# A two-layer model's second modulation: products on GpSimd, or multiply-adds on VectorE

## The chip, the cores and the metric

The kernel runs on one core of one Trainium2 chip. The metric is the device time of one execution in microseconds (us). The kernel before was timed three times: 3883.1, 3865.46 and 3878.24 us, median 3878.24 us. One more execution, of 3871.71 us, was recorded with the hardware profiler; its span is 3870.0 us and all rows below come from it.

The engines are named as the profile names them: PE is TensorE (matmuls and transposes), PEld its weight loads, DVE is VectorE, ACT is ScalarE, POOL is GpSimd, SP is SyncE, which here issues most DMA transfers. Each engine takes its instructions in one fixed order. L821 is line 821 of the kernel.

## The reference, cut to what matters

512 tokens of width 1024 go through two layers. Both end in a mixture of experts with 16,384 experts. The second layer is modulated by a vector `c`, and its attention is partly a differential one:

```python
mod = jax.nn.silu(c) @ w_ada + b_ada              # c: 1024, w_ada: 1024 x 6144
sh1, sc1, g1, sh2, sc2, g2 = split(mod, 6)        # six rows of 1024
h = rms_norm(x, norm1_g) * (1 + sc1) + sh1
proj = h @ w_in                                   # attention inputs and gate logits gl
...
a = softmax(q1 k1^T / 8) - lam * softmax(q2 k2^T / 8)     # 8 heads, 512 x 512 each
ob = rms_norm(a @ v, subln_g) * (1 - lam_init)
gates = sigmoid(gl + b_gate)
x = x + g1 * (mixed @ w_out)
h2 = rms_norm(x, norm2_g) * (1 + sc2) + sh2
x = x + g2 * experts(h2)
```

Only the making of `mod` is touched. Its rows sh1, sc1 and g1 (0 to 2) are made early, beside the first layer's mixture of experts; rows sh2, sc2 and g2 (3 to 5) beside the differential attention. They are first read after that attention has ended.

## The kernel before, in words

**A modulation row** is a product of a vector with a 1024 x 1024 block of `w_ada`. `modulation` (L788) does it without PE for the most part. It loads the block in eight pieces of 128 x 1024 (tile `war`, 512 KB each, two buffers in turn), multiplies each piece with one column of silu(c) (tile `cc`, one value a partition) and adds it into the tile `am`. Then `finish` (L797) sums `am` over the partitions by eight small matmuls against a column of ones (`pmod`, L800), adds the bias (`bada`, L803), turns the result by one transpose (`ptmod`, L806) and stores it to DRAM (`modd`, L809). There is one buffer of `am` and one of `bada`, so a row's first piece can't be written before the matmuls of the row before it have read `am`.

The function has two ways to form `am`. With `on_pool` false a piece takes one DVE instruction, a tensor-scalar product for the first piece (L823) and a fused multiply-add for the other seven (L825), and SP issues the loads. With `on_pool` true POOL issues the loads (L816), and a piece takes a product (L819) and, from the second piece on, a sum (L821), both on POOL. The first call (rows 0 to 2, L1423) is of the first kind, the second call (rows 3 to 5, L1655) of the second.

**The differential attention** (L1608) runs eight times, over four blocks of 128 tokens and two halves of four heads. A pass splits its queries in a high and a low part (`qbhi`, `qblo`), and for each head and each of the two softmaxes makes scores by three matmuls of 512 columns (`bps`, L118 to L120), a row maximum on DVE (`nm`, L746) and an exponential on ACT (`pe`, L748). DVE scales and subtracts the two (L1627, L1630), PE transposes the difference (`bpt`, L1633), ACT copies it, and PE multiplies it with the values (`bpo`, L1637). A normalization follows, whose last step is the only other POOL instruction of the stage (L1646).

Each pass is followed in the program by `projT` (L1590), which makes 256 columns of the gate logits: eight weight pieces of 128 x 256 (`wr`, three buffers) are loaded by SP, split by ACT and DVE in two parts (`wh`, `wl`, L76 and L77), and used by 48 matmuls of 512 columns (`mt`, L1601 to L1603). After each pass the loop asks the modulation for four steps (L1660).

**The order of the work.** The program is written in this order, but a scheduler lays each engine's instructions out anew, by its own estimate of when their inputs will be there. So the gate matmuls stand between the attention's, on PE, and the splits between the softmax steps, on DVE. The order is fixed when the kernel is built. What runs after the stage (sigmoids of the gates, the projections, the second mixture of experts) reads the results of all of it.

Of the kernel before, what the change touches and what calls it, by code (L numbers as in the profile page):

```python
# [23 lines left out]
def build(tc, I, out, dbg=None, stop=None):  # L24
# [763 lines left out]
    def modulation(rows, pool, psum, tags, ptag, on_pool):  # L788

        cc = pool.tile([128, 8], F32, name="cc", bufs=1)  # L790
        S.dma_start(out=cc, in_=I["c_2"])
        A.activation(out=cc, in_=cc, func=AF.Silu)
        ones = pool.tile([128, 1], F32, name="ones", bufs=1)
        G.memset(ones, 1.0)
        mv = modd.rearrange("(i d) -> i d", d=128)

        def finish(i, am):  # L797
            pm = psum.tile([128, 8], F32, name="pmod", tag=ptag)
            for j in range(8):
                T.matmul(pm[:, j:j + 1], am[:, j * 128:(j + 1) * 128], ones, start=True, stop=True)  # L800
            b8 = pool.tile([128, 8], F32, name="bada", tag="bada", bufs=1)
            S.dma_start(out=b8, in_=I["k_bada"][:, i * 8:i * 8 + 8])
            V.tensor_tensor(out=b8, in0=pm, in1=b8, op=OP.add)  # L803
            yield
            pt = psum.tile([128, 128], F32, name="ptmod", tag=ptag)
            T.transpose(pt[0:8, :], b8, ident)  # L806
            mrow = pool.tile([8, 128], F32, name="mrow", tag="mrow", bufs=1)
            A.copy(out=mrow, in_=pt[0:8, :])
            S.dma_start(out=mv[i * 8:i * 8 + 8], in_=mrow)  # L809
            yield  # L810

        for i in rows:
            am = pool.tile([128, 1024], F32, name="am", tag=tags[0])
            for k in range(8):
                raw = pool.tile([128, 1024], F32, name="war", tag=tags[1], bufs=None if tags[1] == "row" else 2)
                (G if on_pool else S).dma_start(out=raw, in_=I["w_ada_2"][k * 128:(k + 1) * 128, i * 1024:(i + 1) * 1024])  # L816
                ck = cc[:, k:k + 1]
                if on_pool:
                    G.tensor_tensor(out=raw if k else am, in0=raw, in1=ck.broadcast_to([128, 1024]), op=OP.mult)  # L819
                    if k:  # L820
                        G.tensor_tensor(out=am, in0=am, in1=raw, op=OP.add)  # L821
                elif k == 0:
                    V.tensor_scalar(out=am, in0=raw, scalar1=ck, scalar2=None, op0=OP.mult)  # L823
                else:
                    V.scalar_tensor_tensor(out=am, in0=raw, scalar=ck, in1=am, op0=OP.mult, op1=OP.add)  # L825
                yield
            for _ in range(ML):
                yield
            yield from finish(i, am)
# [12 lines left out]
    MR = (0, 1, 2)  # L842
# [809 lines left out]
        return f  # L1652

    modp = dp.enter_context(tc.tile_pool(name="modp", bufs=1))
    mods = modulation(tuple(range(len(MR), 6)), modp, pst, ("am", "war"), "tr", True)  # L1655
    for t in range(NT):
        for h4 in range(2):
            differential(t, h4)
# [220 lines left out]
```

## Time and profile before

| | |
|---|---|
| median of three runs | 3878.24 us (3865.46 to 3883.1) |
| the profiled execution | 3871.71 us |
| its span | 3870.0 us |
| the stage of the change, from PE's first `bps` to the last row's `ptmod` | 2183.8 to 2430.8 us, 247.0 us |
| PE busy in the span | 3667.4 us (95%) |
| DVE, POOL busy in the span | 3028.6 us (78%), 1915.2 us (49%) |

The profile is one execution, cut in several ways: busy time by engine, groups of instructions by line with their mean duration, what each engine waited for, and the instructions in order of time. PE's matmuls overlap, and their ends are modelled, so a PE that counts as busy may still run below its peak; for its progress the count of its instructions in a stretch is the better measure. The granted clock (PEclk) is the share of full speed that PE was given in a stretch.

### The profile page before, as it was taken

The numbers are of one execution on the slowest core, as the hardware profiler recorded it, in microseconds if no ns is written. First come the engines' busy times: TensorE is split into PE (matmuls) and PEld (weight loads), VectorE is DVE, ScalarE is ACT, GpSimd is POOL, SyncE is SP. The second block draws the span as 40 slices with busy tenths as digits, with TensorE's granted clock in tenths as the row PEclk, the third lists the DMA queues.
The fourth block names the chain that finished last, engine by engine and source line by source line (L and its number), as shares of the span: only waits on it lengthen the run. The fifth ranks groups of instructions, "written<-read, shape, count | busy, mean of one in ns | idle before, by whom it ended". The sixth has DMA issues, their size and how long they took to land. (4 is left out here: it accounts for less than half of the span.)

```text
span 3870.0 us, 53220 instructions
## 1 busy us (share of the span) xinstructions
PE 3667.4 (95%) x19062; PEld 3166.8 (82%) x19062; DVE 3028.6 (78%) x5530; ACT 1654.5 (43%) x2567; POOL 1915.2 (49%) x1261
## 2 busy tenths in 40 slices
PE   6999999899999999999899988999899999999999
PEld 4777788788899999987777666788788899999987
DVE  8557479996898888877756566589996898888775
ACT  3455433475333333333444566433474333333333
POOL 3000047514778887740524443147524778877740
PEclk8999999999999999999999989999999999999999
DMA  3423132257999899987222322432257999999884
GB/s 110 108 91 120 55 120 88 95 217 266 324 335 327 318 321 322 325 300 249 81 80 65 93 75 71 134 112 88 93 219 271 325 337 327 321 317 323 306 280 147
DMA packets 333513, 789.03 MB, mean 204 GB/s; under 512 B 32432, under 2 KB 152320, under 8 KB 329856
## 3 DMA queue, kind: packets, MB, share of 16 engines
q1 hardware_dynamic: 256064, 504.58, 39.6%
q0 software_dynamic: 77184, 281.05, 20.3%
q8 instruction: 150, 2.46, 0.3%
q14 instruction: 115, 0.94, 0.1%
HBM read 725.34 MB, written 59.01 MB: 203 GB/s over the span
## 5 line engine op out<-in xcount | busy, mean ns | idle before, releaser
L1104 POOL TENSOR_TENSOR ul<-ur,uh 128x1024 fp32r<-128x1024 f32 x256 | 696.3, 2720 | 436.6 <-PE pa L1114 251.5
L1111 PE MATMUL pa<-phi,uh 128*128 128x384 f32 x2048 | 698.1, 341 | 1.5 <-ACT ga L1116 1.5
L1112 PE MATMUL pa<-plo,uh 128*128 128x384 f32 x2048 | 695.7, 340 | 0.0
L1305 PE MATMUL y<-vh,wh 128*128 128x512 f32 x1536 | 596.7, 393 | 15.6 <-ACT wh L1274 13.8
L1306 PE MATMUL y<-vl,wh 128*128 128x512 f32 x1536 | 600.3, 392 | 5.6 <-DVE vl L1276 5.6
L1307 PE MATMUL y<-vh,wl 128*128 128x512 f32 x1536 | 602.4, 394 | 0.0
L1276 DVE TENSOR_TENSOR vl<-vr,vh 128x1024 fp32r<-128x1024 f32 x256 | 359.5, 1404 | 210.6 <-ACT vh L1275 182.6
L1274 ACT CAST wh<-w 128x384 fp32r<-128x384 f32 x256 | 131.4, 513 | 764.1 <-PE y L1306 523.9
L1251 DVE SCALAR_TENSOR_TENSOR acc<-vrow,act,acc 128x1024 f32<-128x1024 f32 x256 | 408.4, 1595 | 56.5 <-DMA vrow<-in_peer_v_dram,ei 28.4
L1240 DVE SCALAR_TENSOR_TENSOR urow<-urow,hgat 128x1024 f32<-128x1024 f32 x256 | 407.6, 1599 | 29.2 <-DMA urow<-in_peer_u_dram,ei 17.2
L1114 PE MATMUL pa<-phi,ul 128*128 128x384 f32 x2048 | 402.8, 339 | 16.5 <-POOL ul L1104 16.4
L1098 ACT CAST uh<-ur 128x1024 fp32r<-128x1024 f32 x256 | 269.6, 1053 | 317.6 <-issue 211.1
L1111 PEld LDWEIGHTS pa<-phi,uh 128*128 128x128 f32 x2048 | 389.3, 190 | 10.2 <-ACT ga L1116 1.9
L1112 PEld LDWEIGHTS pa<-plo,uh 128*128 128x128 f32 x2048 | 389.1, 190 | 9.0
L1114 PEld LDWEIGHTS pa<-phi,ul 128*128 128x128 f32 x2048 | 362.2, 190 | 18.4 <-POOL ul L1104 18.4
L1305 PEld LDWEIGHTS y<-vh,wh 128*128 128x128 f32 x1536 | 289.3, 189 | 72.4 <-ACT wh L1274 14.4
L1307 PEld LDWEIGHTS y<-vh,wl 128*128 128x128 f32 x1536 | 289.9, 189 | 65.3 <-DVE wl L1277 1.9
L1306 PEld LDWEIGHTS y<-vl,wh 128*128 128x128 f32 x1536 | 290.3, 189 | 64.2 <-DVE vl L1276 7.8
L77 DVE TENSOR_TENSOR wl<-wr,wh 128x512 fp32r<-128x512 f32 (+1 forms) x276 | 199.8, 732 | 143.6 <-ACT wh L76 143.5
L1275 ACT CAST vh<-vr 128x1024 fp32r<-128x1024 f32 x256 | 267.7, 1046 | 33.2 <-DMA vr<-in_peer_v_dram 16.0
L1273 DVE TENSOR_TENSOR w<-gbuf,ga 128x384 f32<-128x384 f32 x256 | 214.7, 841 | 38.0 <-issue 18.7
L76 ACT CAST wh<-wr 128x512 fp32r<-128x512 f32 (+1 forms) x276 | 149.2, 551 | 200.1 <-PE mm L120 125.9
(537 smaller groups left out, 7378.9 us busy)
## 6 DMA issues: line engine op xcount, KB each, us to landing
vr<-in_peer_v_dram SPq DMA_DIRECT2D x128, 512.0 KB
ur<-in_peer_uT_dram SPq DMA_DIRECT2D x128, 512.0 KB
vr<-in_expert_v_dram SPq DMA_DIRECT2D x128, 512.0 KB
ur<-in_expert_uT_dram SPq DMA_DIRECT2D x128, 512.0 KB
gbuf<-Gd SPq DMA_DIRECT2D x64, 768.0 KB
Gd<-stg SPq DMA_DIRECT2D x24, 1920.0 KB
wr<-in_w_in_dram SPq DMA_DIRECT2D x104, 256.0 KB
war<-in_w_ada_dram SPq DMA_DIRECT2D x24, 512.0 KB
```

The lines of the kernel that those rows point to most:

```text
L1098: A.copy(out=uh, in_=ua[e])
L1104: G.tensor_tensor(out=ul, in0=raw, in1=uh.bitcast(F32), op=OP.subtract)
L1111: T.matmul(pa, uh[:, k, :], hi[:, k, 0:NDT], start=(k == 0), stop=False)
L1112: T.matmul(pa, uh[:, k, :], lo[:, k, 0:NDT], start=False, stop=False)
L1114: T.matmul(pa, ul[:, k, :], hi[:, k, 0:NDT], start=False, stop=(k == 7))
L1240: V.scalar_tensor_tensor(out=row, in0=row, scalar=1.0, in1=hg_, op0=OP.mult, op1=OP.mult, accum_out=act[:, k:k + 1])
L1251: V.scalar_tensor_tensor(out=acc, in0=rows_.pop((1, k)), scalar=act[:, k:k + 1], in1=acc, op0=OP.mult, op1=OP.add)
L1275: A.copy(out=vh, in_=vr)
L1276: V.tensor_tensor(out=vl, in0=vr, in1=vh.bitcast(F32), op=OP.subtract)
L1305: T.matmul(y[t][c], wh[:, ts], vh[:, cs_], start=(e_ == 0), stop=False)
L1306: T.matmul(y[t][c], wh[:, ts], vl[:, cs_], start=False, stop=False)
L1307: T.matmul(y[t][c], wl[:, ts], vh[:, cs_], start=False, stop=(e_ == 127))
```

## The change

The last argument of the second call goes from true to false. By that the 24 loads of rows 3 to 5 are issued by SP and not by POOL, and the 24 products and 21 sums of POOL are replaced by 3 products and 21 multiply-adds on DVE. The tiles and their buffers stay as they are.

```diff
     modp = dp.enter_context(tc.tile_pool(name="modp", bufs=1))
-    mods = modulation(tuple(range(len(MR), 6)), modp, pst, ("am", "war"), "tr", True)
+    mods = modulation(tuple(range(len(MR), 6)), modp, pst, ("am", "war"), "tr", False)
     for t in range(NT):
         for h4 in range(2):
             differential(t, h4)
```

The lines that the argument chooses between:

```python
(G if on_pool else S).dma_start(out=raw, in_=I["w_ada_2"][...])                     # L816
if on_pool:
    G.tensor_tensor(out=raw if k else am, in0=raw, in1=ck.broadcast_to([128, 1024]), op=OP.mult)
    if k:
        G.tensor_tensor(out=am, in0=am, in1=raw, op=OP.add)
elif k == 0:
    V.tensor_scalar(out=am, in0=raw, scalar1=ck, scalar2=None, op0=OP.mult)
else:
    V.scalar_tensor_tensor(out=am, in0=raw, scalar=ck, in1=am, op0=OP.mult, op1=OP.add)
```

The scheduler lays the stage out anew. On every engine the orders differ only from the start of the stage (from the pieces of row 3 on) to its end. First, DVE at the start of the stage, behind the first pass's query split (`qblo`); the kernel before:

```order
L77 TENSOR_TENSOR qblo<-qbT,qbhi 128x512
L77 TENSOR_TENSOR wl<-wr,wh 128x256 x3
L746 TENSOR_REDUCE nm<-bps 128x1
L77 TENSOR_TENSOR wl<-wr,wh 128x256
L746 TENSOR_REDUCE nm<-bps 128x1
L1624 RECIPROCAL bz<-bz 128x2
```

and the changed kernel at the same place:

```order
L77 TENSOR_TENSOR qblo<-qbT,qbhi 128x512
L77 TENSOR_TENSOR wl<-wr,wh 128x256
L823 TENSOR_SCALAR am<-war,cc 128x1024
L77 TENSOR_TENSOR wl<-wr,wh 128x256
L825 SCALAR_TENSOR_TENSOR am<-war,cc,am 128x1024 x2
L77 TENSOR_TENSOR wl<-wr,wh 128x256
L825 SCALAR_TENSOR_TENSOR am<-war,cc,am 128x1024
L746 TENSOR_REDUCE nm<-bps 128x1 x2
L77 TENSOR_TENSOR wl<-wr,wh 128x256 x2
L825 SCALAR_TENSOR_TENSOR am<-war,cc,am 128x1024 x2
```

Four of row 3's eight pieces stand ahead of the first row maximum; the other four follow before the next pass's query split.

Second, DVE one pass later than the bias of row 3 (`bada`), where most of row 4's pieces stand in the changed kernel, around the next query split:

```order
L77 TENSOR_TENSOR wl<-wr,wh 128x256
L825 SCALAR_TENSOR_TENSOR am<-war,cc,am 128x1024
L746 TENSOR_REDUCE nm<-bps 128x1 x2
L825 SCALAR_TENSOR_TENSOR am<-war,cc,am 128x1024 x2
L1624 RECIPROCAL bz<-bz 128x2
```

and in the kernel before at the same place:

```order
L77 TENSOR_TENSOR wl<-wr,wh 128x256
L746 TENSOR_REDUCE nm<-bps 128x1 x2
L1644 TENSOR_REDUCE bss<-bsq 128x4
L57 TENSOR_SCALAR rbv<-bss 128x4
L59 TENSOR_SCALAR rbh<-rbv 128x4
```

The row's last pieces stand between the row maxima and the reciprocals of the softmax; the first two pieces of rows 4 and 5 stand directly behind the bias of the row before.

Third, SP's issues around the second load of `bada`. Before:

```order
L113 DMA wr<-in_w_in_dram 128x256 x29
L802 DMA bada<-in_k_bada_dram 128x8
L809 DMA modd<-mrow 8x128
L113 DMA wr<-in_w_in_dram 128x256 x23
L802 DMA bada<-in_k_bada_dram 128x8
```

and now:

```order
L113 DMA wr<-in_w_in_dram 128x256 x18
L802 DMA bada<-in_k_bada_dram 128x8
L816 DMA war<-in_w_ada_dram 128x1024
L809 DMA modd<-mrow 8x128
L816 DMA war<-in_w_ada_dram 128x1024
L113 DMA wr<-in_w_in_dram 128x256 x3
L816 DMA war<-in_w_ada_dram 128x1024 x2
L113 DMA wr<-in_w_in_dram 128x256 x2
L816 DMA war<-in_w_ada_dram 128x1024
L113 DMA wr<-in_w_in_dram 128x256 x3
L816 DMA war<-in_w_ada_dram 128x1024 x3
```

The 24 loads of `war` now stand between the gate weights' loads; the two ahead of each second and third `bada` are already the next row's, one `war` load for each buffer.

## Rows read from the trace of the kernel before

**Rows 1.** The page, part 1: busy time, share of the span, instructions.

```profile
PE 3667.4 (95%) x19062; PEld 3166.8 (82%) x19062; DVE 3028.6 (78%) x5530; ACT 1654.5 (43%) x2567; POOL 1915.2 (49%) x1261
```

**Rows 2.** Busy time by stretch of the differential stage; the first row names the columns.

```profile
core 0: us, PE busy (x) PEld busy (x) DVE busy (x) ACT busy (x) POOL busy (x), PEclk, DMA share, GB/s
2183.80:2224.00 40.20, 31.19 (x137) 22.47 (x137) 33.10 (x47) 19.91 (x40) 33.70 (x21) 0.87 0.40 121
2224.00:2272.00 48.00, 47.85 (x245) 34.92 (x243) 28.11 (x76) 42.16 (x85) 2.20 (x3) 0.99 0.16 47
2272.00:2322.00 50.00, 37.51 (x146) 25.55 (x146) 36.25 (x62) 26.61 (x51) 38.97 (x25) 0.80 0.32 101
2322.00:2369.00 47.00, 46.57 (x235) 33.72 (x236) 27.35 (x72) 36.56 (x74) 1.14 (x2) 0.96 0.17 48
2369.00:2410.50 41.50, 31.67 (x140) 22.13 (x139) 31.51 (x49) 23.53 (x49) 35.36 (x21) 0.88 0.34 102
2410.50:2430.80 20.30, 20.10 (x114) 15.63 (x113) 12.24 (x40) 16.93 (x33) 1.04 (x1) 1.00 0.36 107
```

**Rows 3.** POOL's groups of instructions in the whole stage: count, busy us, mean ns, idle before.

```profile
L821 POOL TENSOR_TENSOR am<-am,war 128x1024 f32<-128x1024 f32 x21 | 51.1, 2434 | 1.2
L819 POOL TENSOR_TENSOR war<-war,cc 128x1024 f32<-128x1024 f32 x20 | 40.2, 2010 | 13.9 <-DMA war<-in_w_ada_dram 13.8
```

**Rows 4.** Timeline of DVE and POOL: start us, us, engine, line, operation.

```profile
2191.15 0.42 DVE L77 TENSOR_TENSOR wl<-wr,wh 128x256 fp32r<-128x256 f32 x1
...
2191.50 1.88 POOL L819 TENSOR_TENSOR war<-war,cc 128x1024 f32<-128x1024 f32 x1 [0.56 <-DMA war<-in_w_ada_dram]
2191.56 2.11 DVE L77 TENSOR_TENSOR wl<-wr,wh 128x256 fp32r<-128x256 f32 x1
```

**Rows 5.** DVE's groups, shapes apart, from 2226 to 2270 us.

```profile
L746 DVE TENSOR_REDUCE nm<-bps 128x1 f32<-128x512 f32 x15 | 10.3, 689 | 11.3 <-PE bps L120 11.3
L77 DVE TENSOR_TENSOR wl<-wr,wh 128x256 fp32r<-128x256 f32 x17 | 6.6, 418 | 0.0
L1630 DVE SCALAR_TENSOR_TENSOR pe<-pe,bz 128x512 f32<-128x512 f32 x8 | 6.0, 746 | 0.7 <-ACT pe L1629 0.7
```

**Rows 6.** The same for 2180 to 2222 us (first row) and 2274 to 2322 us.

```profile
L77 DVE TENSOR_TENSOR wl<-wr,wh 128x256 fp32r<-128x256 f32 x10 | 13.1, 1306 | 8.2 <-ACT wh L76 8.2
...
L77 DVE TENSOR_TENSOR wl<-wr,wh 128x256 fp32r<-128x256 f32 x7 | 8.9, 1275 | 0.0
L1630 DVE SCALAR_TENSOR_TENSOR pe<-pe,bz 128x512 f32<-128x512 f32 x4 | 7.8, 1951 | 0.0
L746 DVE TENSOR_REDUCE nm<-bps 128x1 f32<-128x512 f32 x11 | 7.4, 684 | 11.1 <-PE bps L120 11.1
```

**Rows 7.** Waits in the stage: who waited for whom, total us, times, longest.

```profile
DVE nm L746 <- PE bps L120: 41.9, 27, 4.0
...
PE bpt L1633 <- DVE pe L1630: 27.3, 7, 5.3
```

**Rows 8.** Tile war beside the first mixture: ns min/median/max, first and last start.

```profile
L816 SPq DMA_DIRECT2D war<-in_w_ada_dram x24: 327/328/524, 1606.9 to 1780.8; - x24
...
L825 DVE SCALAR_TENSOR_TENSOR am<-war,cc,am x21: 1277/1280/1286, 1717.4 to 1785.4; 128x1024 f32<-128x1024 f32 x21
...
L823 DVE TENSOR_SCALAR am<-war,cc x3: 746/749/753, 1716.6 to 1763.6; 128x1024 f32<-128x1024 f32 x3
```

**Rows 9.** Timeline of POOL: a load's issue and the product that waits for it.

```profile
2218.25 0.59 POOL L816 DMA_DIRECT2D war<-in_w_ada_dram  x1 [0.30 <-POOL am L821]
2222.27 1.89 POOL L819 TENSOR_TENSOR war<-war,cc 128x1024 f32<-128x1024 f32 x1 [3.43 <-DMA war<-in_w_ada_dram]
```

**Rows 10.** Timeline of PE: where the stage begins and where it ends.

```profile
2183.82 0.51 PE L118 MATMUL bps<-kbhi,qbhi 64*128 64x512 f32 x2
...
2430.86 0.27 PE L806 MATMUL ptmod<-ident,bada 128*8 128x128 f32 x1 [0.26 <-DVE bada L803]
```

## The prediction

> **What bounds the kernel now.** I read the page's busy shares first, then busy time by stretch, then groups, waits and single instructions within the stage that the change touches.
>
> Over the whole span PE is busy 95% [rows 1], so an edit pays only where PE is held up. The stage runs from PE's first score matmul at 2183.8 us to the last row's transpose at 2430.8 us [rows 10], 247.0 us. [rows 2] cut it where POOL starts and stops. In three stretches POOL is busy 33.7 of 40.2, 39.0 of 50.0 and 35.4 of 41.5 us: it makes one modulation row in each. In the three between (48.0, 47.0 and 20.3 us) it is nearly idle. PE starts 245 + 235 + 114 = 594 instructions in 115.3 us without POOL, 5.15 a us, and 137 + 146 + 140 = 423 in 131.7 us with it, 3.21 a us. Without POOL PE is busy all but 0.8 us and the granted clock is 0.96 to 1.00; with it PE is idle 9.0 + 12.5 + 9.8 = 31.3 us and the clock is 0.80 to 0.88.
>
> Why is seen on DVE. Beside POOL a weight split of 256 columns takes 1306 or 1275 ns, without it 418; the subtraction of the two softmaxes takes 1951 ns against 746 [rows 5, 6]. The row maximum takes 684 and 689, the same in both. Single instructions show how [rows 4]: a split takes 0.42 us just before a POOL product; the next one starts 0.06 us behind that product and ends 0.29 us after it, having lasted 2.11 us. So certain DVE instructions wait until a POOL instruction has ended. PE pays: its transposes wait 27.3 us for the subtraction L1630, in only 7 waits [rows 7]. In the stretches without POOL DVE is the one that waits, most for scores from PE (11.3 us in 44) [rows 5].
>
> The Trainium skill names this in "SBUF — State Buffer", section "Who interferes with whom": DVE and GpSimd share one pair of ports under an exclusive lock, a DVE instruction with two SBUF inputs loses against a GpSimd instruction that reads SBUF, and a reduction never contends. The trace agrees in all three (2.11 us, 1951 ns, 684 against 689). By that rule the time to be given back is DVE's locked time, 100.9 us busy in the three stretches less 59% of 85.7 us, about 50 us, an estimate from the page's rule and [rows 2]; the sum below would end 4 us lower by it.
>
> **The change part by part.** *Removed: POOL's 24 products and 21 sums* (2.0 and 2.4 us each, 91.3 us for the 41 shown) [rows 3], and its 24 load issues (0.59 us each [rows 9]). POOL's own time costs nothing; the gain is what DVE and PE get back. Bounds: only PE's 31.3 us of idle time comes back; or PE runs the 423 instructions at 5.15 a us, 82.1 us instead of 131.7, a gain of 49.6. A middle way adds to the idle time what the low clock cost while PE was busy: 0.13 x 31.2 + 0.20 x 37.5 + 0.12 x 31.7 = 15.4 us, together 46.7. I take **-46 us**, since the count also mixes long and short matmuls. What is late next is PE itself: the stage would take 201 us, eight passes of 25.
>
> *Added: 3 products and 21 multiply-adds on DVE.* The same lines on the same shapes ran beside the first mixture: 749 and 1280 ns [rows 8]. 3 x 0.75 + 21 x 1.28 = 29.1 us, 9.7 a row. The cover is DVE's idle time: without POOL it is busy 28.1 + 27.4 + 12.2 = 67.7 of 115.3 us, 59%, which leaves 10 us in a pass of 25. But the changed order puts a whole row in little more than one pass, 9.7 us into some 11, so DVE is about full there, and it takes its work in order: behind a multiply-add stand row maxima, reciprocals and the subtraction that PE's transposes wait for. Ends: nothing where it fits the gaps, 29.1 us where all of it delays PE. With DVE nearly full I take half, **+14.5 us**.
>
> *Added: waits of DVE for the loads.* Two buffers serve the eight pieces, so from the third on a load is issued only after the multiply-add two pieces back has ended. From POOL such a load took 4.0 us from issue to use (2218.25 to 2222.27) [rows 9]; from SP I assume the same, since the trace shows it only with other loads around. The order leaves other DVE work in between: only the last piece of each row has less than 4 us of it (1.28 us of the piece before and about 1.4 of two row maxima), so some 1.5 us a row are waited for. The first two pieces of rows 4 and 5 are loaded a whole row ahead. The wait also holds row maxima; as above I count a third, **+1.5 us** in all. The ends are 0 and, if each of 18 pieces waits its 4 us, 72.
>
> *Moved: 24 loads to SP*, 0.33 us each [rows 8], 7.9 us in 247 on a queue that issues 64 small weight loads here. A `war` load that waits for its buffer holds the weight loads behind it, but three weight buffers are ahead, and each serves six matmuls. Nothing, if the multiply-adds come in time; else it is part of the 72.
>
> *Moved: nothing else.* The loads carry the same bytes. POOL's remaining instruction L1646 is read after the stage. Behind the stage every engine's order is the same, so the rest of the kernel shifts as a whole.
>
> Sum: -46 + 14.5 + 1.5 = **-30 us**. 3871.7 - 30 = 3841.7 for an execution like the profiled one, which ran 6.5 us under the median; against the median 3848 us.
>
> **The rivals.** *All of the added work fits DVE's gaps.* For it: 41% of DVE's time is free. Against it: a row within one pass. The gain is 46 us or a little more: 3832.
>
> *DVE becomes the bound of each row.* All 29.1 us and a wait of about 1 us at each of the 18 later pieces come onto the path, some 46 us, and cancel the gain: 3878, no change. For it: 98% booking in those passes and an order made from estimates; against it: PE's transposes had only 7 long waits even with DVE's instructions at two to three times their length.
>
> *The loads pace DVE, and DVE paces PE.* Two buffers, an SP queue in which `war` and weight loads wait for each other's buffers, and a DVE that stops at each piece: 18 x 4.0 = 72 us exposed, and 14.5 of work, less 46: +40, 3918. It decides from the point where a piece waits more than (46 - 14.5) / 18 = 1.75 us on the path. For it: POOL too waited 13.8 us for these loads [rows 3]; against it: the spacing in the order, worked out above.
>
> *Not POOL but the load traffic slows DVE.* The DMA share is 0.32 to 0.40 beside POOL and 0.16 where it rests. Then the stretches stay slow and the 29.1 us come on top: half of it, +14.5, 3893. Against it: from 2410.5 us the DMA share is 0.36, PE busy 20.1 of 20.3 us and the clock 1.00 [rows 2].
>
> **How the numbers follow.** A measurement of this kernel tells about 0.5% from no change, 19 us here. The forecast (19 to 42 us gained) gets 0.52, the work hidden altogether 0.13, DVE as the bound 0.23, the pacing by loads 0.10, the traffic 0.02. Faster by over 0.5%: 0.52 + 0.13 = 0.65; within: 0.23; slower: 0.12. The range goes from 3829 (all hidden, and 3 us of the count's larger bound) to 3880 (all of DVE's work exposed); it leaves out the slower cases and a little below. The likeliest case alone is 3836 to 3859.
>
> **What would show it.** Right: in the changed profile the stage is 215 to 220 us; splits and subtractions take 0.42 and 0.75 us throughout; the granted clock is above 0.95 in most of it; PE's waits for L1630 fall to a third; L825 takes 1.28 us. The half that I charge shows as PE idle behind DVE in the first, the fourth to fifth and the seventh to eighth pass. Wrong: L825 with long waits for `war` (the loads pace), splits that stay above 1 us (the traffic), or a stage that saves its locked time and is no shorter (DVE as the bound). A stage under 205 us would say that nothing had to be paid.

## The result and the profile after

The changed kernel takes 3834.5 us (median of 6 runs, 3830.3 to 3840.3) against 3879.7 us for the kernel before in the same comparison (6 runs, 3865.5 to 3883.5). The ratio is 0.9889 with a 95% interval of 0.9871 to 0.9908, so 36 to 50 us are gained. The forecast was 3848, a gain of 30 us, with a range of 3829 to 3880: direction and mechanism of the gain held, its size was too small by some 15 us. In the profiled execution (3833.36 us, span 3831.6 us) the stage goes from 2190.28 us to the transpose at 2390.66 us, 200.4 us against 247.0 [rows 10], 46.6 less.

Busy time by stretch in the changed kernel, cut where VectorE's multiply-adds start and stop; the first row names the columns, and [rows 2] is its counterpart:

```profile
core 0: us, PE busy (x) PEld busy (x) DVE busy (x) ACT busy (x) POOL busy (x), PEclk, DMA share, GB/s
2190.30:2210.00 19.70, 18.50 (x89) 12.97 (x89) 17.23 (x32) 12.17 (x28) 0.00 (x0) 1.00 0.64 195
2210.00:2267.00 57.00, 57.00 (x299) 40.41 (x296) 34.14 (x97) 49.18 (x95) 2.08 (x2) 1.00 0.16 49
2267.00:2296.00 29.00, 28.91 (x142) 19.98 (x142) 26.03 (x59) 24.28 (x51) 1.09 (x1) 1.00 0.54 167
2296.00:2341.80 45.80, 45.80 (x241) 32.51 (x240) 28.40 (x84) 39.19 (x76) 2.08 (x2) 1.00 0.19 57
2341.80:2370.00 28.20, 28.20 (x137) 19.42 (x136) 25.72 (x57) 22.71 (x46) 1.09 (x1) 1.00 0.49 150
2370.00:2390.70 20.70, 20.44 (x116) 15.70 (x114) 12.54 (x40) 17.23 (x34) 1.04 (x1) 1.00 0.35 109
```

A modulation row is now made in the first, third and fifth stretch. DVE is nearly full there (17.2 of 19.7, 26.0 of 29.0, 25.7 of 28.2 us), and still PE is idle 1.2, 0.1 and 0.0 us and its granted clock is 1.00, the upper of its two levels (2.4 GHz). Before, with POOL making the row, PE was idle 9.0, 12.5 and 9.8 us and the mean clock was 0.80 to 0.88 [rows 2].

DVE's groups in the stage after (count, busy us, mean ns, idle before), which answer to [rows 5, 6]:

```profile
L746 DVE TENSOR_REDUCE nm<-bps 128x1 f32<-128x512 f32 x64 | 43.1, 687 | 27.0 <-PE bps L120 26.8
L825 DVE SCALAR_TENSOR_TENSOR am<-war,cc,am 128x1024 f32<-128x1024 f32 x20 | 27.2, 1359 | 5.2 <-DMA war<-in_w_ada_dram 5.0
L77 DVE TENSOR_TENSOR wl<-wr,wh 128x256 fp32r<-128x256 f32 x62 | 24.7, 416 | 2.3 <-ACT wh L76 2.1
L1630 DVE SCALAR_TENSOR_TENSOR pe<-pe,bz 128x512 f32<-128x512 f32 x32 | 23.8, 745 | 0.2
L1627 DVE TENSOR_SCALAR pe<-pe,bz 128x512 f32<-128x512 f32 x16 | 7.7, 482 | 0.2
```

Splits take 416 ns and subtractions 745 over the whole stage, the durations that before were found only where POOL rested. So DVE is busy 144.1 us in the stage, less than the sum of [rows 2], 168.6, although some 29 us of work were added. All that is left of PE's waits in the stage (total us, times, longest):

```profile
PE bps L118 <- ACT pe L748: 1.2, 1, 1.2
...
PE ptmod L806 <- DVE bada L803: 0.3, 1, 0.3
```

The wait for L1630, 27.3 us [rows 7], is gone altogether.

### The profile page after: what moved, and what is told of

Read it like the earlier page. It is cut to its first block, busy times and chain, and to the rows that moved or that the text cites. A ratio compares the mean times of both kernels' runs of the same rounds, so it can differ in the third digit from the quotient of the medians.

```text
span 3831.6 us, 53218 instructions
## 1 busy us (share of the span) xinstructions
PE 3659.9 (96%) x19062; PEld 3158.1 (82%) x19062; DVE 2999.7 (78%) x5554; ACT 1653.4 (43%) x2567; POOL 1802.3 (47%) x1192
## 4 chain that ended last, share of the span: by engine, by line
PE 71%; DVE 15%; DMA 5%; ACT 4%; issue 3%; POOL 2%; SPq 1%; DVEq 0%; POOLq 0%; ACTq 0%
PE y L1305 8%; PE y L1307 8%; PE y L1306 8%; PE pa L1114 7%; PE pa L1112 7%; PE pa L1111 7%; PE pgg L1213 4%; PE mm L119 3%; PE mm L120 3%; PE mm L118 3%; DVE E L968 2%; ACT stg L1214 2%; PE mt L1603 1%; PE mt L1601 1%; DVE eq L959 1%
## 5 line engine op out<-in xcount | busy, mean ns | idle before, releaser
L1104 POOL TENSOR_TENSOR ul<-ur,uh 128x1024 fp32r<-128x1024 f32 x256 | 695.5, 2717 | 435.6 <-PE pa L1114 261.1
L1114 PE MATMUL pa<-phi,ul 128*128 128x384 f32 x2048 | 403.1, 340 | 15.9 <-POOL ul L1104 15.8
L77 DVE TENSOR_TENSOR wl<-wr,wh 128x512 fp32r<-128x512 f32 (+1 forms) x276 | 177.9, 653 | 142.4 <-ACT wh L76 142.1
L76 ACT CAST wh<-wr 128x512 fp32r<-128x512 f32 (+1 forms) x276 | 149.4, 550 | 209.3 <-PE mm L120 129.2
```

The source lines that it names most:

```text
L1104: G.tensor_tensor(out=ul, in0=raw, in1=uh.bitcast(F32), op=OP.subtract)
L1114: T.matmul(pa, ul[:, k, :], hi[:, k, 0:NDT], start=False, stop=(k == 7))
```

## The experiments

One measure serves all runs: from PE's first score matmul to its last transpose of this stage, in which before, after and seven of the runs start the same 982 PE instructions, as the trace counts them. The row of before, then of after:

```profile
2183.80:2426.30 242.50, 210.59 (x982) 150.70 (x981) 168.40 (x341) 161.27 (x319) 112.41 (x71) 0.91 0.27 83
```

```profile
2190.30:2386.10 195.80, 194.52 (x982) 137.21 (x981) 143.80 (x363) 160.32 (x319) 7.39 (x7) 1.00 0.33 100
```

So the measure says 242.5 and 195.8 us. Of the 46.7 us between them 30.6 are idle time of PE (31.9 before, 1.3 after) and 16.1 are time for which PE counted as busy longer with as many instructions, at a mean clock of 0.91 and not 1.00 (210.6 against 194.5). All runs, each ratio to runs of the kernel before made beside it (their medians go from 3875.7 to 3881.8 us):

| run | median us | ratio to before, 95% | stage us |
|---|---|---|---|
| before | 3879.7 | 1 | 242.5 |
| changed | 3834.5 | 0.9889 (0.9871 to 0.9908) | 195.8 |
| loads by GpSimd | 3841.3 | 0.9907 (0.9888 to 0.9926) | 205.3 |
| arithmetic by GpSimd | 3885.7 | 1.0019 (1.0002 to 1.0035) | 249.8 |
| one piece of each row | 3831.9 | 0.9884 (0.9866 to 0.9903) | 196.6 |
| multiply-adds doubled | 3843.8 | 0.9909 (0.9883 to 0.9936) | 204.7 |
| GpSimd reads beside | 3856.2 | 0.9948 (0.9929 to 0.9966) | 225.3 |
| GpSimd fills beside | 3832.4 | 0.9894 (0.9868 to 0.9920) | 199.9 |
| rope on VectorE too | 3817.8 | 0.9851 (0.9828 to 0.9874) | 197.6 |
| query split on VectorE | 3861.1 | 0.9951 (0.9935 to 0.9967) | 196.7 |
| rope and norm on VectorE | 3821.2 | 0.9852 (0.9830 to 0.9875) | 199.7 |
| changed, again | 3833.5 | 0.9876 (0.9852 to 0.9900) | 196.1 |

**Only the loads back on GpSimd.** Two theories stood: GpSimd's arithmetic blocks VectorE, or the load traffic and its queue do.

```diff
-                (G if on_pool else S).dma_start(out=raw, ...)
+                (G if tags[1] == "war" else S).dma_start(out=raw, ...)
```

> The multiply-adds stay on VectorE as in the changed kernel; only the 24 loads of rows 3 to 5 are issued by GpSimd again. Theory (GpSimd's arithmetic on SBUF blocks VectorE): the stage stays at 198 to 206 us and the time at 3834 +- 10; splits L77 stay near 420 ns, subtractions L1630 near 750 ns. Rival (the load traffic, or that GpSimd's queue drives it, slowed VectorE): the stage goes back to 235 to 250 us, 3870 to 3885, with splits above 1000 ns beside the loads.

Measured: 3841.3 us, stage 205.3. Splits took 417 ns and subtractions 746, so nothing of the blocking came back, and nearly all of the gain stayed. Yet the stage is 9.5 us longer than in the changed kernel (209.8 us to the last row's transpose, a little over the 198 to 206 expected):

```profile
2192.60:2397.90 205.30, 198.10 (x982) 139.57 (x981) 144.81 (x363) 160.29 (x319) 18.16 (x27) 0.98 0.32 96
```

PE is idle 7.2 us, by the waits all of it behind ScalarE: 4.7 us in 2 waits for a copied transpose (L1635) and 2.5 for an exponential (L748). That is 5.9 us more than in the changed kernel, and PE counts as busy 3.6 us longer, with the mean clock at 0.98. DVE waits 8.5 us in 8 times for `war` at L825 (5.5 in 5 after), and its splits of 256 columns 6.0 us for L76 (2.1 after). The new issuer also moved some of PE's instructions in its order. Later loads or the other order: these two were not told apart.

**Only the arithmetic back on GpSimd.** The other half; here PE and DVE have the order of before.

```diff
-                (G if on_pool else S).dma_start(out=raw, ...)
+                S.dma_start(out=raw, ...)
...
-    mods = modulation(tuple(range(len(MR), 6)), modp, pst, ("am", "war"), "tr", False)
+    mods = modulation(tuple(range(len(MR), 6)), modp, pst, ("am", "war"), "tr", True)
```

> The other half: SyncE issues the loads, GpSimd makes the products and sums as before; PE's and VectorE's order are the same as before the change. Theory (GpSimd's arithmetic): nothing of the gain, stage 243 to 251 us, 3880 +- 10, splits and subtractions beside GpSimd at 1300 and 1950 ns. Rival (GpSimd's loads or the queue they stand in): stage 200 to 215 us, 3835 to 3848.

Measured: 3885.7 us, stage 249.8. Nothing of the gain is left, so the move of the loads alone brought none of it, and the rival on the traffic falls. The stage is even 7 us longer than before (254.3 us to the last row's transpose, over the 243 to 251 expected). PE's waits in it (total us, times, longest):

```profile
PE bpt L1633 <- DVE pe L1630: 26.8, 9, 6.5
...
PE bps L118 <- ACT pe L748: 6.0, 3, 3.2
```

PE's wait for the subtraction is as in [rows 7] (27.3), and there is more for the exponentials (6.0; 1.0 in the stage before). What is new is that SP, which also issues the weight loads, stands behind GpSimd's sums for a free buffer; that this made the 7 us was not tried.

```profile
SPq L816 <- POOL am L821: 56.5, 15, 5.8
```

**The added work taken away.** Rows 3 to 5 from their first piece alone leave out 21 loads and 21 multiply-adds, and with them most of what the rows should sum.

```diff
-            for k in range(8):
+            for k in range(1 if tags[1] == "war" else 8):
```

> Of the changed kernel, rows 3 to 5 are made from their first piece alone, so that 21 loads of 512 KB and 21 multiply-adds (26.9 us of VectorE at 1.28 us each) are left out. Theory one (the added work lies wholly in VectorE's gaps): the stage is within 3 us of the changed kernel's 200 us, time within 5 us of it. Theory two (half of it is on the path, as the prediction charged): the stage falls to 184 to 190 us, time about 14 us under the changed kernel's. Theory three (all of it): 171 to 176 us.

Measured: 3831.9 us, stage 196.6, against 195.8 and 196.1 in the two profiles of the changed kernel. Theory one: 26.9 us of VectorE's work and 21 loads cost little or nothing. DVE's busy time fell by 21.5 us, and the stage did not:

```profile
2194.60:2391.20 196.60, 195.69 (x999) 139.90 (x999) 122.33 (x344) 160.29 (x320) 7.34 (x7) 0.99 0.16 46
```

The stage holds 17 PE instructions more here, since the last row's small matmuls now come before its end; by their durations they take some 2 us. PE's order differs in hundreds of places as well. So the price of the added work is 0 to 3 us, and no finer. The changed kernel's own row bounds it too: PE is idle there 1.3 us at a clock of 1.00.

What was freed turned into waits of DVE for PE and ScalarE, here and then in the changed kernel (2190 to 2402 us in both; total us, times, longest):

```profile
DVE nm L746 <- PE bps L120: 38.9, 35, 3.1
DVE bz L1624 <- ACT pe L748: 19.1, 15, 2.8
DVE wl L77 <- ACT wh L76: 10.1, 6, 4.5
```

```profile
DVE nm L746 <- PE bps L120: 26.8, 30, 3.0
DVE bz L1624 <- ACT pe L748: 13.4, 12, 2.3
...
DVE wl L77 <- ACT wh L76: 2.1, 4, 0.5
```

**The added work doubled.** Where does the cover end?

```diff
                     V.scalar_tensor_tensor(out=am, in0=raw, scalar=ck, in1=am, op0=OP.mult, op1=OP.add)
+                    if tags[1] == "war":
+                        V.scalar_tensor_tensor(out=raw, in0=raw, scalar=ck, in1=am, op0=OP.mult, op1=OP.add)
```

> Each of the 21 multiply-adds of rows 3 to 5 is followed by a second one of the same shape whose result is not used: 26.9 us more on VectorE, and each buffer comes free 1.28 us later. Theory one (hidden in gaps that hold it again): 200 to 204 us, time within 5 us of the changed kernel's. Theory two (half of added work is paid): +13.5 us, stage 214, 3848. Theory three (the cover has an end: in the windows of rows 4 and 5 VectorE is busy 26.0 of 29.0 and 25.7 of 28.2 us in the changed kernel, so some 3 us a row are left): about 9 - 3 = 6 us a row are paid, +18 us, stage 218, 3852, with PE idle behind VectorE in these windows alone.

Measured: 3843.8 us, stage 204.7, or 211.1 instead of 200.4 to the last row's transpose. So the profile is 9 to 11 us longer, less than either theory with a price. The four executions go from 3832.2 to 3849.0 us, and the lowest is within the changed kernel's own spread. DVE hardly waits for `war` any more (1.0 us at L825) and is busy 165.0 of the 204.7 us. Two rows of 5 us each from the third modulation row:

```profile
2352.00:2357.00 5.00, 5.00 (x12) 3.48 (x12) 5.00 (x10) 2.96 (x7) 0.00 (x0) 0.50 0.44 116
...
2377.00:2382.00 5.00, 4.24 (x23) 3.19 (x22) 5.00 (x9) 3.81 (x7) 0.00 (x0) 1.00 0.57 193
```

In the second PE is idle 0.8 us beside a full DVE. In the first PE counts as busy but runs at half the clock, its lower level (1.2 GHz), and starts 12 instructions. Over the stage PE is idle 2.0 us, only 0.7 more than in the changed kernel, so the idle time behind VectorE that theory three asked for did not come. The low clock cost about 3.5 us (0.87, 0.50 and 0.94 in three rows of 5 us); the rest of the 9, some 5 us, is not located. PE's order differs from the changed kernel's in hundreds of places too. So it is not shown that VectorE's second helping of work is what costs the 9 us.

**GpSimd reads, with no role in the result.** The changed kernel, in which GpSimd beside two of the rows multiplies and adds a tile that nobody needs; PE's and DVE's orders are those of the changed kernel, row for row.

```diff
+        jk = ob[:, 3, :] if tags[1] == "war" else None
+        if jk is not None:
+            G.memset(jk, 0.0)
...
+                if jk is not None and i < 5:
+                    G.tensor_tensor(out=jk, in0=jk, in1=cc[:, 0:1].broadcast_to([128, 1024]), op=OP.mult)
+                    if k:
+                        G.tensor_tensor(out=jk, in0=jk, in1=jk, op=OP.add)
```

> The changed kernel (VectorE makes the rows, SyncE loads them, the order of PE and VectorE is the same word for word), and beside rows 3 and 4 GpSimd makes 16 products and 14 sums of 128x1024 on a tile that nobody reads: some 64 us of GpSimd arithmetic that reads SBUF, with no load, no wait and no result in it. Measured from the first score matmul to the last transpose of the stage, 195.7 us in the changed kernel, 242.4 before. Theory (arithmetic on GpSimd alone blocks VectorE): 46.7 us x 64 / 91 = 33 us come back, if VectorE's added work beside it costs nothing more; 222 to 240 us, splits beside GpSimd above 1200 ns. Rival (GpSimd slowed VectorE through its loads or as a link in a chain of waits): 195 to 202 us.

Measured: 3856.2 us, stage 225.3: 29.5 us come back. Of the 65.5 us of GpSimd work 59.5 lie within the stage, so 0.50 us are paid for each; the kernel before lost 46.7 for 94.0 us of products and sums within its stage, 0.50 too. This also answers a rival that the other runs leave open, that the gain came from the new order of the instructions: here the order is the changed kernel's, and with GpSimd beside two of the three rows about two thirds of the gain are lost. DVE's groups in the stage, in which L828 and L1637 are what L825 and L1630 were:

```profile
L746 DVE TENSOR_REDUCE nm<-bps 128x1 f32<-128x512 f32 x64 | 43.0, 686 | 26.1 <-PE bps L120 26.0
L77 DVE TENSOR_TENSOR wl<-wr,wh 128x256 fp32r<-128x256 f32 x64 | 39.9, 641 | 3.3 <-ACT wh L76 3.3
L828 DVE SCALAR_TENSOR_TENSOR am<-war,cc,am 128x1024 f32<-128x1024 f32 x21 | 38.9, 1853 | 2.2 <-DMA war<-in_w_ada_dram 2.0
L1637 DVE SCALAR_TENSOR_TENSOR pe<-pe,bz 128x512 f32<-128x512 f32 x32 | 30.3, 947 | 0.2
```

**GpSimd writes.** The same, with fills in place of products and sums.

```diff
-                    G.tensor_tensor(out=jk, in0=jk, in1=cc[:, 0:1].broadcast_to([128, 1024]), op=OP.mult)
-                    if k:
-                        G.tensor_tensor(out=jk, in0=jk, in1=jk, op=OP.add)
+                    for _ in range(5 if k else 2):
+                        G.memset(jk, 0.0)
```

> The same as the run with products and sums beside it, with fills of the same tile in their place: 74 of 128x1024, 0.96 us each as such a fill took elsewhere in the kernel, 71 us of GpSimd work that writes SBUF and reads nothing. Theory one (what blocks is GpSimd's reading, for VectorE's instructions with two inputs in SBUF): splits L77 and subtractions L1630 stay near 420 and 750 ns, at most the one-input L1627 (482 ns) is longer; the stage 195 to 203 us. Theory two (any GpSimd access blocks VectorE): as with products and sums, 222 us and more.

Measured: 3832.4 us, stage 199.9. The fills and DVE's groups in the stage (L1636 is the subtraction):

```profile
L831 POOL MEMSET ob<- 128x1024 f32 x60 | 57.9, 964 | 3.4
...
L828 DVE SCALAR_TENSOR_TENSOR am<-war,cc,am 128x1024 f32<-128x1024 f32 x20 | 27.2, 1360 | 6.2 <-DMA war<-in_w_ada_dram 6.0
L77 DVE TENSOR_TENSOR wl<-wr,wh 128x256 fp32r<-128x256 f32 x62 | 25.0, 421 | 1.8 <-ACT wh L76 1.7
L1636 DVE SCALAR_TENSOR_TENSOR pe<-pe,bz 128x512 f32<-128x512 f32 x32 | 23.9, 746 | 0.2
...
L1633 DVE TENSOR_SCALAR pe<-pe,bz 128x512 f32<-128x512 f32 x16 | 9.0, 560 | 0.2
```

58 us of GpSimd fills in the stage leave splits and subtractions as they were; only the one-input L1627 (L1633 here) grows, from 482 to 560 ns, 1.3 us in all. Theory one: what blocks is GpSimd's arithmetic that reads SBUF, not its writing. A GpSimd copy, which reads and does no arithmetic, was not tried. The stage is 4 us longer in this profile, which has a granted clock of 0.66 from 2194.3 to 2204.3 us, near the start; the time of the kernel does not show it.

**Three further moves from GpSimd.** First the rope's products and sum, ahead of the stage:

```diff
-            G.tensor_tensor(out=ro, in0=ro, in1=ra, op=OP.add)
+            V.tensor_tensor(out=ro, in0=ro, in1=ra, op=OP.add)
```

(and L1469 and L1470 in the same way).

> On top of the changed kernel the rope's two products and one sum (L1469 to L1471), 96 instructions and 98.5 us of GpSimd between 1880 and 2190 us, go to VectorE as well. If the lesson carries (a GpSimd product costs PE what it blocks on VectorE, and VectorE has room): PE's waits of 9.4 us for L1472 go, VectorE's L1468 and L1472 shorten by their blocked time; 5 to 12 us gained, 3822 to 3830. If VectorE's 24 x (0.87 + 0.71) us there grow by some 60 us of new work beyond its gaps: 3835 to 3850.

Measured: 3817.8 us (3814.6 to 3818.4), 16 to 17 us under the changed kernel (10 to 15 by the ratios to before) and better than expected; it is the fastest version here. From 1880 to 2110 us, after and then this run:

```profile
1880.00:2110.00 230.00, 217.89 (x1153) 177.15 (x1152) 138.16 (x283) 98.86 (x194) 86.42 (x90) 0.97 0.25 71
```

```profile
1880.00:2110.00 230.00, 227.40 (x1223) 183.32 (x1224) 154.10 (x416) 107.00 (x211) 0.00 (x0) 1.00 0.26 73
```

GpSimd's 86.4 us become 15.9 us more of DVE, since L1468 falls from 873 to 702 ns and the moved sum takes 684 instead of 1484. PE is idle 2.6 us instead of 12.1 and starts 70 instructions more; its wait for L1472 falls from 9.4 to 2.0 us. Here the stage begins at 2169.9 us, 20 earlier than in the first profile of after.

Then the query projection's split:

```diff
-            G.tensor_tensor(out=wl, in0=raw, in1=wh.bitcast(F32), op=OP.subtract)
+            V.tensor_tensor(out=wl, in0=raw, in1=wh.bitcast(F32), op=OP.subtract)
```

> On top of the changed kernel the 32 splits L869 of 128x1024 (2.43 us each on GpSimd, 77.8 us) are made by VectorE. PE waits 9.4 us in 5 times for them in the changed kernel. If VectorE makes one in about 1.4 us between its other work there: 5 to 10 us gained, 3825 to 3830. If VectorE has no room there: 0 to 20 us lost.

Measured: 3861.1 us, 27 us lost, more than expected. On DVE the split takes 1205 to 2582 ns, and PE waits longer for it than for GpSimd's (9.4 us in 5 times):

```profile
PE pa L1114 <- POOL ul L1104: 23.1, 6, 6.8
PE pq L878 <- DVE qwl L869: 21.0, 8, 4.1
```

GpSimd's own splits L1104 are waited for 23.1 us instead of 15.8. The two waits grow by 18.9 us, most of what was lost. They suggest that such a move pays only where DVE comes to it in time; no further run tried that.

Last, on top of the rope, the norm's eight products L1646 within the stage, `G.tensor_tensor` replaced by `V.tensor_tensor` as above:

> On top of the run with the rope on VectorE, the 8 products L1646 (1.04 us each on GpSimd, 8.4 us), the last GpSimd work within the stage, go to VectorE too. In the stage PE is busy 198.9 of 200.4 us in the changed kernel, so nothing is held up any more: if a GpSimd product costs only where PE waits behind VectorE, the time is within 4 us of that run's 3818. If every GpSimd product costs what it blocks: 4 to 8 us gained, 3810 to 3814. If VectorE's order suffers: 3822 and more.

Measured: 3821.2 us, stage 199.7, no gain over 3817.8: with GpSimd silent in the stage nothing more comes back; PE was idle there only 1.6 us before the move.

**The changed kernel again.**

> The changed kernel once more, unaltered, for a second profile on the chip of the run beside it. Theory: from the first score matmul to the last transpose 193 to 198 us again (195.7 in the first profile); the 6.5 us by which that profile's stage began later than before's (2190.3 against 2183.8 us) come and go between executions of the same code, and the stage begins anywhere from 2183 to 2195. Rival: the later start belongs to the change, and it begins at 2190 +- 1 again.

Measured: 3833.5 us, stage 196.1, begin 2194.4 us. With the two other kernels of the same PE and DVE order (2193.1 and 2184.3) the begin varies by 10 us between executions; before's own order began at 2183.8 us, and at 2193.1 with the arithmetic by GpSimd. So the 6.5 us ahead of the stage in the first profile of after need be no effect of the change.

## Why the prediction was right in kind and too small in size

*POOL's lock removed, -46 us: right.* The stage lost 46.6 us, between the ends 31.3 and 49.6 and on the middle way that added the low clock to PE's idle time. The two parts came as they were taken: 31.3 us of idle time and 15.4 of low clock there, 30.6 and 16.1 in the rows of before and after. The two halves undone show that the arithmetic carries it: with it back nothing is gained, with the loads alone back most of the gain stays. The two runs with unused work beside the rows show that it is arithmetic that reads SBUF, and not fills, without any link to the result.

The Trainium skill, "SBUF — State Buffer", section "Who interferes with whom", says that a VectorE instruction with two SBUF inputs contends with a GpSimd instruction that reads SBUF and not with one that only writes it. The runs agree on both counts: 641 ns beside reads and 421 beside fills for the mean split, 416 without either. That section of the Trainium skill lets a one-input `tensor_scalar` contend as well in some modes; the 482 and 560 ns of L1627 would fit that. Where the prediction says that VectorE's instruction loses, the runs show both sides waiting: GpSimd waits in turn, as the rows of the last section show.

*Added work on DVE, +14.5 us: this is the step that failed, and with it the sum.* "The added work taken away" measures it: 0 to 3 us. The prediction saw rightly that DVE would be nearly full in each row's window, but then charged half of the work because a row puts "9.7 us into some 11" and DVE takes its work in order. Fullness is not yet lateness. DVE had waited 41.9 us for PE's scores [rows 7]; after, it still waits 26.8 us for them, 6.2 us in 2274 to 2322 us alone. The run with the work taken away shows the exchange: 21.5 us less work, and 12.1 + 5.7 + 8.0 us more waiting in the three rows above. A multiply-add took from waits for scores, exponentials and rounded weights that would have stood there, and PE hardly felt it. Where this cover ends is not shown: with the work doubled the profile is 9 to 11 us longer, but hardly any of it as PE idle behind VectorE.

*Waits for the loads, +1.5 us: more waits than expected, and nothing paid for them.* DVE waited 7.2 us in 6 times for `war` (some 4.5 were expected in three rows), 5.8 of it in the first row. Landing took 3.7 to 8.2 us over the 48 loads of the run, median 4.2, and 3.7 to 4.8 in the stage, against the 4.0 that were assumed. PE paid nothing for the waits that shows. The multiply-add took 1.28 us in the median, as it should, and 1.36 in the mean of the stage, with one of 2.06:

```profile
L816 SPq DMA_DIRECT2D war<-in_w_ada_dram x48: 327/328/455, 1609.3 to 2361.2; - x48
L825 DVE SCALAR_TENSOR_TENSOR am<-war,cc,am x42: 1266/1279/2059, 1719.0 to 2366.8; 128x1024 f32<-128x1024 f32 x42
...
  DMA war<-in_w_ada_dram: 7.2, 6
...
DMA to landing us min/median/max: 3.7/4.2/8.2
```

*What would show it.* Splits of 0.42 and subtractions of 0.75 us in the mean of the stage, a clock above 0.95 and L825 at 1.28 us in the median came as said. The stage of 215 to 220 us did not, nor did the third of PE's waits for L1630: none was left. The prediction's own sign for this, a stage under 205 us when nothing has to be paid, was met by 200.4. The rival that came out is the first one (all of the added work fits), at 3832, which had a chance of 0.13. The likeliest case, 19 to 42 us gained, did not come; the measured 45 lie within the range because the range reached as far as this rival.

*The other rivals.* DVE as the bound of each row and DVE paced by the loads are refuted by PE's idle times of 1.2, 0.1 and 0.0 us. Yet the second has a trace: with GpSimd as the issuer the stage is 9.5 us longer at only 3 us more of waiting for `war`; why so much is open.

## What to carry to other kernels

Price a GpSimd instruction that reads SBUF by what it does to VectorE's two-input instructions beside it, and then only where TensorE waits behind VectorE: here about half a microsecond per microsecond of GpSimd, nothing for fills, and nothing more to be had in the stage once TensorE was full. Before charging work put on an engine, look whether that engine waits for the bound engine nearby: here those waits were the cover, even at 90% busy. Check each such move by itself, for the same step gained 16 us in one stage and lost 27 in another.

## What the runs showed of the hardware

- A GpSimd product or sum on SBUF can hold a two-input VectorE instruction for its whole length (a split of 2.11 us beside a product of 1.88 us [rows 4]), and a fill does not: 58 us of fills moved the mean split from 416 to 421 ns, 65.5 us of products and sums to 641.
- GpSimd is held in turn: in the run with products and sums seven of them that began 1.0 us before the end of a VectorE multiply-add took 2.75 or 2.76 us, and five that began beside no two-input instruction 1.89 or 1.90. One of the seven (start us, us):

```profile
2194.22 2.80 DVE L828 SCALAR_TENSOR_TENSOR am<-war,cc,am 128x1024 f32<-128x1024 f32 x1
...
2196.01 2.76 POOL L832 TENSOR_TENSOR ob<-ob 128x1024 f32<-128x1024 f32 x1
```

- The granted clock can fall to its lower level (0.50, 2352 to 2357 us of the doubled run) although PE counted as busy through the 15 us before, 93 instructions, with the clock at 1.00, 1.00 and 0.87 in them; no run here says why.
